# A two-layer decoder trunk on one core: block sums placed behind chosen relus, finished pairs turned earlier, and another order of the last products, roots and stores

## The chip, the cores and the metric

The kernel runs on one core of a Trainium2 chip, as a single program. The metric is the device time of the program in microseconds (us); shorter is better. The time before is the median of three runs, and one further execution was taken by the hardware profiler. An instruction belongs to one of five engines, which the profile calls PE (TensorE), DVE (VectorE), ACT (ScalarE), POOL (GpSimd) and SP (SyncE, which here only issues transfers). Each engine works through its own instructions in the order in which they were built; a scheduler fixes that order at build time, and semaphores tie the engines together.

## What is computed

The reference is a decoder trunk of two layers on 512 tokens of 1024 values, in float32:

```
for layer in range(2):
    h = rms_norm(x, norm_mix[layer])
    x = x + (short_conv_mixer(h, ...) if layer == 0 else nsa_mixer(h, ..., shared))
    x = x + squared_relu_mlp(rms_norm(x, norm_mlp[layer]), mlp_w1[layer], mlp_w2[layer])
    if layer == 0:
        shared = nsa_shared_kv(rms_norm(x, kv_norm), ...)
return rms_norm(x, final_norm)

def squared_relu_mlp(h, w1, w2):          # w1: 1024 x 4096, w2: 4096 x 1024
    return square(relu(h @ w1)) @ w2
```

The first layer mixes with a short gated convolution, the second with sparse attention over keys and values that are computed once. The change touches the two MLPs and the final norm only.

## The kernel before, in words

**Numbers.** Every float32 operand of a product is split into a high and a low half in float16, and a product is three matmuls (high by high, high by low, low by high). A weight arrives by a transfer into a float32 staging buffer (`wst`); ScalarE makes its high half (`whi`) and VectorE its low half (`wlo`). The residual `X` lies turned, channels on the partitions, in 8 tiles of 128 channels by 512 tokens.

**The MLP.** It is done in two halves of 2048 hidden units. `mlp_up` (L487) computes a half's hidden units in 8 pairs of 128-row tiles. A pair is 48 matmuls of 512 columns (L341 to L343). What follows them is a chain over the engines: two relus on VectorE (L499, with the norm's root as a row `rb` multiplied in), one square on ScalarE (L501), four sums of 128x256 on POOL (L503), the high half `rh` on ScalarE (L504) and the low half `rl` on VectorE (L505). The four sums form the seven combinations in which a 2x2 block product needs only seven products instead of eight; `rh` and `rl` hold all seven for the down products.

`mlp_down` (L538) runs over 4 pairs of output tiles. A pair takes 8 pieces of hidden units, each with 7 products of three matmuls of 256 columns (L550 to L552). The weights come as blocks: a staging buffer holds two pieces, VectorE forms the weights' combinations in place with four sums (L182, the list `W_SUMS`), ScalarE makes the high half of all seven combinations (L184, 128x1792) and VectorE the low half (L185, 128x1792). `combine` (L508) turns the seven sums in PSUM into additions to `X`: one ScalarE copy `dn_p` (L520), two VectorE operations that make `dn_w`, then a generator of seven more VectorE operations, which `mlp_down` advances one step behind every piece of the next pair.

**Which weights are ready when.** All weights stand in one list of pieces in the order of their use. `ahead` (L215) is called behind a pair's weights or a block's first piece; it converts pieces until 2 (for blocks 3) are ready beyond those in use. Staging buffers: 3 for plain pieces and 3 for blocks; converted ones: 4 and 4. `convert_piece` (L171) ends by starting the transfers for which a staging buffer has come free, on SP's queue. So a half's first three blocks are loaded, summed and split while the last up pairs still run. Nothing in the kernel says where among the up pairs they stand on VectorE: the scheduler places them, by when it expects their data and their engine.

**The root of the MLP's norm.** Sums of squares of `X` are gathered while `X` is made; in the first half's first up pair, four small matmuls add them over the partitions, and `rstd_of` (L295 to L305) makes the reciprocal root by a square root on ScalarE and five VectorE operations that refine it. Four transposes (L312) spread it into `rb`, which the first relu needs.

**The end.** In the last down phase (layer 1, half 1) each finished pair of output tiles is turned back to token-major form while the next pair is computed. `mid_b` calls `token_major` (L1168) for both halves of the tokens behind piece 5 of the next pair: TensorE transposes (L1166), ScalarE squares with an accumulating sum (L1162), ScalarE copies (L1177) into `xt` (the tiles `xsh` and `xsl`, 4 x 128 tokens), and POOL multiplies by the final norm's gain (L1178). At that place on ScalarE they stand, in the order built, behind the conversions of four blocks. The last output pair is `last_b` (L1205): its seven products are run one behind the other, each with its own additions (through the helper `stt`, L1213), then the last transposes, and `store` (L1188) makes two tokens tiles' root, scales them with ScalarE (L1195) and VectorE, and starts the transfer to the output on SP's queue (L1203): one per 128 tokens, whole rows.

The order on TensorE is the order of the program's text. Lines of the profile are those of the kernel before.

Of the kernel before, what the change touches and what calls it, by code (L numbers as in the profile page):

```python
# [48 lines left out]
def body(ctx, tc, x, rel_bias, norm_mix, norm_mlp, mlp_w1, mlp_w2, a_w_in, a_conv_w, a_w_out,  # L49
# [121 lines left out]
    def convert_piece(step=1024):  # L171
# [7 lines left out]
        if shape is None:  # L179
            b = t.rearrange("p (k b n) -> p k b n", k=2, n=128)  # L180
            for e, o, x, y in W_SUMS:
                DVE.tensor_tensor(b[:, :, o], b[:, :, x], b[:, :, y], op=e)  # L182
# [303 lines left out]

    def mlp_up(xs, ss, rh, half, rb):  # L487
        turn[0] = 1
        for p in range(8):
# [8 lines left out]
            for m in range(2):  # L498
                DVE.scalar_tensor_tensor(t[:, m], ph[m], 0.0, rb, op0=OP.max, op1=OP.mult)  # L499
# [6 lines left out]
        return rb  # L506

    def combine(p, acc7, done):  # L508
# [11 lines left out]
        ACT.activation(p1, P1, AF.Copy, scale=sc)  # L520
# [17 lines left out]
    def mlp_down(rh, done, mid=None, last=None):  # L538

        post = iter(())  # L540
        for p in range(4):
# [13 lines left out]
            for c in range(0, 4 if late else 8, 2):  # L555
                w = next_piece()
                for k in range(2):
                    for i in range(7):
                        product(i, c + k, [u[:, k] for u in w])
                    if c + k == 5 and mid:  # L560
                        mid(p)
                    if k == 0:
                        drain(ahead())
                    next(post, None)
# [8 lines left out]
            post = combine(p, acc7, done)  # L573
        drain(post)
# [570 lines left out]
    with pool("hidden_b") as hp:  # L1145
# [22 lines left out]
        def token_major(p, h, tag):  # L1168
# [4 lines left out]
            for i in range(2):  # L1173
# [3 lines left out]
                ACT.activation(o, v, AF.Copy)  # L1177
                POOL.tensor_tensor(o, o, gains(p), op=OP.mult)  # L1178

        def mid_b(p):  # L1180
            if p:
                for h in range(2):
                    token_major(p - 1, h, "a" if p % 2 else "c")
# [4 lines left out]
        def store(h, late=None):  # L1188
            sst = work.tile([128, 2], F32, name="sst", bufs=2)
            DVE.tensor_reduce(sst, ssf[:, 2 * h:2 * h + 2], axis=mybir.AxisListType.X, op=OP.add)  # L1190
            r = rstd_of(sst)
            for i in range(2):
                t = 2 * h + i
                a, b = xt[t][:, 0:512], xt[t][:, 512:1024]
                ACT.activation(a, a, AF.Copy, scale=r[:, i:i + 1])  # L1195
                if late:
                    b = xt[t][:, 512:768]
                    DVE.scalar_tensor_tensor(xt[t][:, 768:896], late[i], r[:, i:i + 1], gains(3, 1),
                                             op0=OP.mult, op1=OP.mult)
                    c = xt[t][:, 896:1024]  # L1200
                    DVE.tensor_scalar(c, c, r[:, i:i + 1], None, op0=OP.mult)
                DVE.tensor_scalar(b, b, r[:, i:i + 1], None, op0=OP.mult)
                nc.sync.dma_start(out[0, t * 128:(t + 1) * 128, :], xt[t])  # L1203

        def last_b(acc7, product):  # L1205
# [16 lines left out]
            DVE.tensor_tensor(X1[:, n1], X1[:, n1], p1, op=OP.add)  # L1222
# [61 lines left out]
```

## Time and profile before

| what | us |
|---|---|
| median of 3 runs | 1137.51 (1137.13 to 1138.04) |
| the profiled execution's own time | 1136.88 |
| its span, first to last instruction | 1135.1 |
| matmuls of a 512-column tile, mean (L341 to L343) | 0.379 |
| four POOL sums L503, all 128 | 99.9 in all, 0.801 each |
| high halves of blocks on ScalarE L184, 64 | 106.9 in all, 1.692 each |
| low halves of blocks on VectorE L185, 64 | 128.8 in all, 2.019 each |
| weight sums on VectorE L182, 256 | 108.9 in all, 0.469 each |
| `rl` on VectorE L505, 32 | 64.8 in all, 2.026 each |

The page gives each engine's busy time and its share of the span, the span in 40 slices, the transfers, the chain of work that ended last, and the costliest groups of instructions. A row of a timeline is: start and duration in us, engine, line, operation, output <- inputs with their shape and type, how many alike in a row, and in brackets how long the engine was idle just before and what ended that. A duration there is that of the instruction from start to end; two in a row may overlap by about 0.1 us, so "step" below means the distance from one start to the next. A matmul's duration is longer than its step: 512 columns take 0.38 from start to end, and follow each other every 0.22. Times in the text that name no row are differences of such starts.

### The profile page before, as it was taken

Reading aid. Unit: us, or ns where it says so; the run is one execution under the profiler, and the core shown is the slowest. Engines: PE = TensorE matmul, PEld = TensorE weight load, DVE = VectorE, ACT = ScalarE, POOL = GpSimd, SP = SyncE. Lnnn points to the kernel's source line nnn. Section 1 sums busy time; section 2 is a strip of 40 time slices with the busy share of each in tenths; the row PEclk is TensorE's granted clock in tenths of the full one; section 3 lists DMA queues with packets and bytes.
Section 4 is the critical chain, followed back from the end, with each engine's and each line's share of the span. In section 5 each row is a group of like instructions: output and inputs, shape, how many; then the busy total and the mean of one; then the engine's idle time right before and its main releaser. Section 6 shows DMA issues by size and latency. Waiting matters only on the chain.

```text
span 1135.1 us, 20099 instructions
## 1 busy us (share of the span) xinstructions
PE 1095.8 (97%) x7959; PEld 694.1 (61%) x7959; DVE 832.3 (73%) x1498; ACT 568.5 (50%) x922; POOL 157.6 (14%) x198
## 2 busy tenths in 40 slices
PE   8999999999999999999999989899999999999985
PEld 4444444446884448865767666664444787445874
DVE  4755458765897556999589969896895598754795
ACT  4532235444433444556679777765544433343452
POOL 0000000422000221001002022220122100123020
PEclk9999999999999999999999999999999999999998
DMA  6433335333333333313334341112633333330221
GB/s 210 130 94 97 107 105 172 113 93 113 112 112 112 111 95 107 112 42 120 112 78 122 83 138 38 39 38 74 187 111 112 111 109 115 105 95 7 84 84 75
DMA packets 149378, 115.75 MB, mean 102 GB/s; under 512 B 8612, under 2 KB 146564, under 8 KB 149284
## 3 DMA queue, kind: packets, MB, share of 16 engines
q1 hardware_dynamic: 146736, 109.47, 31.8%
q10 hardware_dynamic: 2260, 4.40, 1.3%
q8 instruction: 62, 1.02, 0.4%
q0 software_dynamic: 288, 0.61, 0.2%
q14 instruction: 32, 0.26, 0.1%
HBM read 110.22 MB, written 2.14 MB: 99 GB/s over the span
## 4 chain that ended last, share of the span: by engine, by line
PE 50%; DVE 19%; ACT 11%; issue 7%; POOL 7%; DMA 5%; SPq 1%; DVEq 0%; ACTq 0%; POOLq 0%
POOL ml_z L503 6%; PE a L341 4%; PE a L342 4%; PE a L343 4%; DVE wlo L185 4%; DMA wst<-mlp_w_dram 3%; ACT rh L504 3%; PE c L343 3%; PE c L342 3%; PE c L341 3%; PE b L342 3%; PE b L341 3%; PE b L343 3%; DVE wlo L196 3%; DVE ml_t L499 2%
## 5 line engine op out<-in xcount | busy, mean ns | idle before, releaser
L195 ACT ACTIVATE whi<-wst 128x1024 f16<-128x1024 f32 (+4 forms) x171 | 142.4, 858 | 127.9 <-PE b L342 38.4
L196 DVE SCALAR_TENSOR_TENSOR wlo<-wst,whi 128x1024 f16<-128x1024 f32 (+4 forms) x171 | 169.9, 1001 | 40.2 <-ACT whi L195 39.9
L503 POOL TENSOR_TENSOR ml_z<-ml_z 128x256 f32<-128x256 f32 x128 | 99.9, 801 | 610.1 <-ACT ml_z L501 410.1
L184 ACT ACTIVATE whi<-wst 128x1792 f16<-128x1792 f32 x64 | 106.9, 1692 | 135.4 <-DVE wst L182 102.3
L341 PEld LDWEIGHTS <-whi 128*128 128x128 f16 x1024 | 100.4, 98 | 112.3 <-issue 5.5
L343 PEld LDWEIGHTS <-wlo 128*128 128x128 f16 x1024 | 100.2, 98 | 112.1 <-issue 0.4
L342 PEld LDWEIGHTS <-whi 128*128 128x128 f16 x1024 | 100.2, 98 | 107.6 <-issue 2.0
L505 DVE TENSOR_TENSOR rl<-ml_z,rh 128x1792 f16<-128x1792 f32 x32 | 64.8, 2026 | 135.9 <-ACT rh L504 135.7
L185 DVE SCALAR_TENSOR_TENSOR wlo<-wst,whi 128x1792 f16<-128x1792 f32 x64 | 128.8, 2019 | 3.0 <-ACT whi L184 2.9
L182 DVE TENSOR_TENSOR wst<-wst 128x256 f32<-128x256 f32 x256 | 108.9, 469 | 24.4 <-DMA wst<-mlp_w_dram 23.4
L504 ACT ACTIVATE rh<-ml_z 128x1792 f16<-128x1792 f32 x32 | 54.3, 1698 | 106.1 <-POOL ml_z L503 106.1
L551 PEld LDWEIGHTS <-whi 128*128 128x128 f16 x896 | 87.7, 98 | 16.2 <-issue 5.6
L552 PEld LDWEIGHTS <-wlo 128*128 128x128 f16 x896 | 87.6, 98 | 15.0 <-issue 4.2
L550 PEld LDWEIGHTS <-whi 128*128 128x128 f16 x896 | 87.7, 98 | 10.5
L343 PE MATMUL b<-xsh,wlo 128*128 128x512 f16 x208 | 78.8, 379 | 0.0
L342 PE MATMUL b<-xsl,whi 128*128 128x512 f16 x208 | 78.8, 379 | 0.0
L341 PE MATMUL b<-xsh,whi 128*128 128x512 f16 x208 | 78.7, 379 | 0.0
L501 ACT ACTIVATE ml_z<-ml_t 128x1024 f32<-128x1024 f32 x32 | 33.8, 1057 | 88.4 <-DVE ml_t L499 88.4
L963 ACT ACTIVATE at_p<-at_s,at_m 128x128 f32<-128x128 f32 (+3 forms) x128 | 71.0, 557 | 13.7 <-DVE at_m L961 12.6
L551 PE MATMUL a<-rl,whi 128*128 128x256 f16 x256 | 69.8, 273 | 3.7 <-DVE rl L505 3.7
L341 PE MATMUL c<-xsh,whi 128*128 128x512 f16 x192 | 72.8, 379 | 0.0
L342 PE MATMUL c<-xsl,whi 128*128 128x512 f16 x192 | 72.8, 379 | 0.0
(309 smaller groups left out, 2686.4 us busy)
## 6 DMA issues: line engine op xcount, KB each, us to landing
wst<-mlp_w_dram SPq DMA_DIRECT2D x256, 256.0 KB, 3.3
wst<-a_w_in_dram SPq DMA_DIRECT2D x18, 512.0 KB, 3.5
wst<-w_kv_dram SPq DMA_DIRECT2D x12, 512.0 KB, 3.5
T<-ext_d ACTq DMA_DIRECT2D x4, 1056.0 KB, 6.0
wst<-a_w_out_dram SPq DMA_DIRECT2D x8, 512.0 KB, 3.4
wst<-b_w_qg_dram SPq DMA_DIRECT2D x8, 512.0 KB, 3.5
wst<-b_w_o_dram SPq DMA_DIRECT2D x8, 512.0 KB, 3.3
wst<-a_w_in_dram SPq DMA_DIRECT2D x8, 384.0 KB, 5.5
```

The lines of the kernel that those rows point to most:

```text
L182: DVE.tensor_tensor(b[:, :, o], b[:, :, x], b[:, :, y], op=e)
L184: ACT.activation(hi, b[:, :, 1:], AF.Copy, scale=sc)
L185: DVE.scalar_tensor_tensor(lo, b[:, :, 1:], sc, hi, op0=OP.mult, op1=OP.subtract)
L195: ACT.activation(hi[:, s:e], w, AF.Copy, scale=sc)
L196: DVE.scalar_tensor_tensor(lo[:, s:e], w, sc, hi[:, s:e], op0=OP.mult, op1=OP.subtract)
L341: PE.matmul(ps, w[0], xs[0], start=start, stop=False)
L342: PE.matmul(ps, w[0], xs[1], start=False, stop=False)
L343: PE.matmul(ps, w[1], xs[0], start=False, stop=stop)
L503: POOL.tensor_tensor(z[:, o], z[:, a], z[:, b], op=e)
L504: ACT.activation(rh[0][:, p], z[:, 1:8], AF.Copy)
L550: PE.matmul(acc7[i], wh, xh, start=c == 0 and not other, stop=False, skip_group_check=other)
L551: PE.matmul(acc7[i], wh, xl, start=False, stop=False, skip_group_check=other)
```

## The change

Four things are changed.

- **Block sums behind a relu.** A list `hold` takes the second relu of up pairs 2, 4 and 6 of each half. When the next block is converted, its four sums are ordered behind the relu that stands first in the list (`issue_after` keeps the order on VectorE; it is no wait). Which operations then follow is again up to the scheduler. There are three relus and three blocks ahead.
- **Finished pairs at once.** In `mlp_down`, the call that converts further weights (`drain(ahead())`) is ordered behind an instruction: at a pair's first piece behind the copy `dn_p` of the pair before (`copied`), and in the last down phase, at piece 5, behind the last copy of the turned tokens (`mid` now returns it). There, the block of pieces 4 and 5 calls it at its second piece instead of its first. `combine` is advanced one step directly when it is made, and no longer at piece 0.
- **The last pair.** `last_b` runs the product for P5 before that for P7, with their additions. The first two token tiles' gain and root are no longer applied by `store`: `root` makes a root, and for tiles 0 and 1 one VectorE operation applies gain and root to the last 256 columns straight from PSUM and another the root to columns 0 to 767; both stand behind the last addition (`final`) on VectorE. ScalarE no longer scales those two tiles.
- **The stores.** `put` starts a transfer: whole rows of tiles 0 and 1 on SP's queue, then tiles 2 and 3 in two halves of the columns, the first on ScalarE's queue behind its scaling, the second on SP's.

```diff
@@ convert_piece
-            for e, o, x, y in W_SUMS:
-                DVE.tensor_tensor(b[:, :, o], b[:, :, x], b[:, :, y], op=e)
+            with tc.issue_after(hold.pop(0).ins) if hold else nullcontext():
+                for e, o, x, y in W_SUMS:
+                    DVE.tensor_tensor(b[:, :, o], b[:, :, x], b[:, :, y], op=e)
@@ mlp_up
+    hold = []
...
-                DVE.scalar_tensor_tensor(t[:, m], ph[m], 0.0, rb, op0=OP.max, op1=OP.mult)
+                relu = DVE.scalar_tensor_tensor(t[:, m], ph[m], 0.0, rb, op0=OP.max, op1=OP.mult)
+            if p in (2, 4, 6):
+                hold.append(relu)
@@ combine
-        ACT.activation(p1, P1, AF.Copy, scale=sc)
+        copied[0] = ACT.activation(p1, P1, AF.Copy, scale=sc)
@@ mlp_down
-                    if c + k == 5 and mid:
-                        mid(p)
-                    if k == 0:
-                        drain(ahead())
-                    next(post, None)
+                    behind = None
+                    if c + k == 0 and p:
+                        behind = copied[0]
+                    if c + k == 5 and mid and p:
+                        behind = mid(p)
+                    if k == (1 if c == 4 and mid else 0):
+                        with tc.issue_after(behind.ins) if behind else nullcontext():
+                            drain(ahead())
+                    if c + k or not p:
+                        next(post, None)
...
             post = combine(p, acc7, done)
+            next(post)
@@ token_major, mid_b
-                ACT.activation(o, v, AF.Copy)
+                last = ACT.activation(o, v, AF.Copy)
                 POOL.tensor_tensor(o, o, gains(p), op=OP.mult)
+            return last
...
-            if p:
-                for h in range(2):
-                    token_major(p - 1, h, "a" if p % 2 else "c")
+            return [token_major(p - 1, h, "a" if p % 2 else "c") for h in range(2)][1]
@@ store becomes root and put
+        def root(h):
+            sst = work.tile([128, 2], F32, name="sst", bufs=2)
+            DVE.tensor_reduce(sst, ssf[:, 2 * h:2 * h + 2], axis=mybir.AxisListType.X, op=OP.add)
+            return rstd_of(sst)
+
+        def put(t, queue, at=slice(0, D)):
+            queue.dma_start(out[0, t * 128:(t + 1) * 128, at], xt[t][:, at])
@@ last_b
+            product(4)
+            stt(both, P5[:, None, :].to_broadcast([128, 2, 256]), both)
             product(3)
             stt(wv[:, 0], P7, wv[:, 1])
             DVE.tensor_tensor(both, both, wv, op=OP.add)
-            product(4)
-            stt(both, P5[:, None, :].to_broadcast([128, 2, 256]), both)
...
-                DVE.tensor_tensor(xt[t][:, 768:1024], ps[:, 0:256], gains(3), op=OP.mult)
-            store(0)
+                early.append(ps[:, 0:256])
+            r = root(0)
...
-                DVE.tensor_tensor(xt[t][:, 896:1024], ps[:, 0:128], gains(3)[:, 128:256], op=OP.mult)
+                early.append(ps[:, 0:128])
             product(6)
-            stt(X2[:, n1], P4, X2[:, n1])
+            final = DVE.scalar_tensor_tensor(X2[:, n1], P4, sc, X2[:, n1], op0=OP.mult, op1=OP.add)
...
-            store(1, late)
+            with tc.issue_after(final.ins):
+                for t in range(2):
+                    DVE.scalar_tensor_tensor(xt[t][:, 768:1024], early[t], r[:, t:t + 1], gains(3),
+                                             op0=OP.mult, op1=OP.mult)
+                    DVE.tensor_scalar(xt[t][:, 0:768], xt[t][:, 0:768], r[:, t:t + 1], None, op0=OP.mult)
+                    put(t, nc.sync)
+            r = root(1)
+            for i in range(2):
+                t, c = 2 + i, r[:, i:i + 1]
+                ACT.activation(xt[t][:, lo], xt[t][:, lo], AF.Copy, scale=c)
+                put(t, nc.scalar, lo)
+                DVE.scalar_tensor_tensor(xt[t][:, 768:896], late[i], c, gains(3, 1), op0=OP.mult, op1=OP.mult)
+                DVE.scalar_tensor_tensor(xt[t][:, 896:1024], early[t], c, gains(3)[:, 128:256],
+                                         op0=OP.mult, op1=OP.mult)
+                DVE.tensor_scalar(xt[t][:, 512:768], xt[t][:, 512:768], c, None, op0=OP.mult)
+                put(t, nc.sync, hi)
```

More of the change, by code (lines that the diff above doesn't have):

```diff
@@ L1 @@
 import math
-from contextlib import ExitStack
+from contextlib import nullcontext, ExitStack
 import numpy as np
@@ L506, in mlp_up @@
         return rb
+    copied = [None]
     def combine(p, acc7, done):
@@ L1232, in last_b @@
             stt(X1[:, n1], P2, X1[:, n1])
+            lo, hi = slice(0, 512), slice(512, 1024)
+            early = []
             for t in range(2):
```

14 lines of the change are left out of this document (removed).

## Prediction

> **What bounds the kernel now.** The page is read first, then the list of what TensorE waited for, then the engines' timelines around each wait.
>
> ```profile
> span 1135.1 us, 20099 instructions
> PE 1095.8 (97%) x7959; PEld 694.1 (61%) x7959; DVE 832.3 (73%) x1498; ACT 568.5 (50%) x922; POOL 157.6 (14%) x198
> ```
>
> TensorE is busy in 97% of the span. The change takes no product away, so it can only move the 39 us in which TensorE is idle, and the end after the last product. The waits of TensorE that lie in the two MLPs:
>
> ```profile
> PE a L551 <- DVE rl L505: 3.7, 3, 1.8
> PE a L550 <- ACT xsh L1177: 2.5, 1, 2.5
> ...
> PE e L312 <- DVE rs_r L305: 1.8, 2, 0.9
> ...
> PE c L1166 <- DVE X L1213: 1.5, 1, 1.5
> ...
> PE c L550 <- DVE dn_w L1213: 0.8, 1, 0.8
> PE a L1166 <- DVE X L531: 0.6, 1, 0.6
> ...
> PE a L550 <- ACT xsl L1177: 0.5, 1, 0.5
> PE c L550 <- ACT xsl L1177: 0.5, 1, 0.5
> PE c L550 <- ACT xsh L1177: 0.4, 1, 0.4
> ```
>
> Columns: waiter, releaser, us in total, times, longest. They sum to 12.3 us; these are what the change can win or make longer. The first row is three of the four turns from the up to the down products; the timeline of VectorE, then of TensorE, shows why.
>
> ```profile
> 264.92 1.28 DVE L499 SCALAR_TENSOR_TENSOR ml_t<-b,rb 128x512 f32<-128x512 f32 x2
> ...
> 272.03 2.03 DVE L505 TENSOR_TENSOR rl<-ml_z,rh 128x1792 f16<-128x1792 f32 x1 [4.70 <-ACT rh L504]
> 273.98 1.22 DVE L196 SCALAR_TENSOR_TENSOR wlo<-wst,whi 128x1024 f16<-128x1024 f32 x1
> 275.11 1.28 DVE L499 SCALAR_TENSOR_TENSOR ml_t<-c,rb 128x512 f32<-128x512 f32 x2
> ```
> ```profile
> 255.83 0.38 PE L343 MATMUL b<-xsh,wlo 128*128 128x512 f16 x1
> ...
> 266.19 0.38 PE L343 MATMUL c<-xsh,wlo 128*128 128x512 f16 x1
> ...
> 282.45 0.27 PE L550 MATMUL a<-rh,whi 128*128 128x256 f16 x1
> 284.31 0.27 PE L551 MATMUL a<-rl,whi 128*128 128x256 f16 x1 [1.58 <-DVE rl L505]
> ```
>
> The relu (L499), square, four POOL sums, `rh` and `rl` (L505) are a chain, and VectorE runs in order, so the next relu stands behind this `rl`. The chain turns once in 10.19 us (264.92 to 275.11), TensorE's pair in 10.36 (255.83 to 266.19). A relu that is late therefore wins back only 0.17 us a pair. Here it starts 8.92 us behind its pair's last product (275.11 - 266.19). `rl` ends 9.15 us after its relu's start (264.92 to 272.03 + 2.03), at 18.1. TensorE has 16.4 us of products that don't need it (to 282.56, one step after 282.45) and waits for the rest. **So the wait at a turn is lag + 9.15 - 16.4**, and each us put into the chain is a us of waiting once the lag is over 7.2.
>
> **Part 1: the block sums.** The built order of the changed program says where they now stand. In each half, behind the relus of pairs 2 and 4: one sum (L182), the up weights' low half, three sums, `rl`, a block's low half (L185), another up low half, the next relu. Behind pairs 3 and 5: four sums before `rl`. Behind pair 6: four sums, `rl`, two block low halves, the last relu. Behind that: eight sums and two up low halves ahead of the last `rl`. Sums fall into VectorE's 4.70 us of idleness, but POOL's sums run in the same time. The rows of POOL in pairs 0, 2 and 3, and of VectorE in pair 2, price that; then the block low halves and sums by themselves:
>
> ```profile
> 201.19 5.64 POOL L503 TENSOR_TENSOR ml_z<-ml_z 128x256 f32<-128x256 f32 x4 [197.56 <-DMA wst<-mlp_w_dram]
> ...
> 226.03 3.47 POOL L503 TENSOR_TENSOR ml_z<-ml_z 128x256 f32<-128x256 f32 x4 [7.96 <-ACT ml_z L501]
> 236.80 2.90 POOL L503 TENSOR_TENSOR ml_z<-ml_z 128x256 f32<-128x256 f32 x4 [7.29 <-ACT ml_z L501]
> ```
> ```profile
> 226.25 4.00 DVE L182 TENSOR_TENSOR wst<-wst 128x256 f32<-128x256 f32 x5
> ...
> 352.77 2.02 DVE L185 SCALAR_TENSOR_TENSOR wlo<-wst,whi 128x1792 f16<-128x1792 f32 x1
> 354.70 1.76 DVE L182 TENSOR_TENSOR wst<-wst 128x256 f32<-128x256 f32 x5
> ```
>
> Five sums take 1.76 us alone and 4.00 beside POOL, whose four go from 2.90 to 3.47: +0.57 in the chain per pair with sums. Its bounds: 0, where they miss each other, and +2.7, the 5.64 of pair 0. I take 0.57, since four of the pairs repeat pair 2's picture. A block low half between `rl` and relu adds its step, 1.93 (352.77 to 354.70). The Trainium skill ("SBUF — State Buffer", Who interferes with whom) says that a VectorE operation with two SBUF inputs and a POOL operation that reads SBUF exclude each other for the whole instruction. The trace agrees (4.00 against 1.76), and the rule speaks against this change; the sum would be the same by it.
>
> Per half: pairs 2 and 4 gain 2 x (0.57 + 1.93) = 5.0, pairs 3 and 5 2 x 0.57 = 1.1. Pair 6: its up low half now stands behind three sums and reaches 1 us into POOL's time (+0.9), two block low halves (+3.9), one up low half fewer before the relu (-1.14, 273.98 to 275.11): +3.6. Less 5 x 0.17: **+8.9 of lag**. The last `rl`: POOL's 0.57, and VectorE, with eight sums and two low halves, is free only at 8.2 us instead of 7.1: +1.1 (half 1, with shorter low halves: +0.8).
>
> What lag do the halves start from? Half 0: the first relu waits for the weights' high half, released by pair 0's last product:
>
> ```profile
> 192.34 1.06 ACT L195 ACTIVATE whi<-wst 128x1024 f16<-128x1024 f32 x1 [3.05 <-PE b L342]
> ```
>
> With its low half (1.22 in the rows above) behind it the relu starts at 194.6, 2.4 behind pair 0's last product, which is issued just ahead of this row; two pairs and the root's four transposes (0.5 of TensorE's time, by the eight of L1166 below) bring pair 2 to 1.6. Turn: 1.6 + 8.9 + 9.15 + 1.1 - 16.4 = **4.4 us**, in each layer. Half 1: the sums of its first blocks leave the end of the down phase and the relu's front (354.70 is one such row), so the lag starts at 0.4, a product's own 0.38. Turn: 0.4 + 8.9 + 9.15 + 0.8 - 16.4 = **2.9**. In layer 1's half 1 pairs 2 to 4 gain 5.6; behind pairs 5 and 6 no up low half follows (-1.14 each), and in pair 6 a block's low half holds POOL's last sum back (1.95), a second one (1.93) and two sums (0.7) precede the relu: -0.6 and +3.4. Lag 0.4 + 5.6 - 0.6 + 3.4 - 0.85 = 8.0, `rl`, with 0.4 of POOL, at 17.6, wait **1.2**. Together 4.4 + 4.4 + 2.9 + 1.2 = 12.9 where 3.7 stood: **+9.2**.
>
> Loads on SP's queue: blocks' loads now stand between up loads, each behind a low half; the up load next in the queue needs the staging buffer of the low half directly behind, so nothing waits longer. POOL's own order doesn't change.
>
> **Part 1b: the root.** Before, a block's low half sits inside the root's chain:
>
> ```profile
> 190.75 0.17 DVE L301 RECIPROCAL rs_r<-rs_r 128x4 f32<-128x4 f32 x1
> 190.83 1.99 DVE L185 SCALAR_TENSOR_TENSOR wlo<-wst,whi 128x1792 f16<-128x1792 f32 x1
> ...
> 193.56 0.15 DVE L305 SCALAR_TENSOR_TENSOR rs_r<-rs_t,rs_r 128x4 f32<-128x4 f32 x1
> ```
>
> Without it and the sums the root is there by 191, before TensorE asks. Both waits for `rs_r` go: **-1.8**; next is TensorE itself.
>
> **Part 2: finished pairs.** In the last down phase ScalarE now copies the turned tokens behind the second conversion instead of the fourth:
>
> ```profile
> 1076.26 3.29 ACT L184 ACTIVATE whi<-wst 128x1792 f16<-128x1792 f32 x2 [3.18 <-DVE wst L182]
> ```
> ```profile
> 1072.79 1.04 PE L1166 MATMUL a<-ident,X 128*128 128x128 f32 x8
> ...
> 1080.87 0.27 PE L550 MATMUL a<-rh,whi 128*128 128x256 f16 x1 [2.46 <-ACT xsh L1177]
> ...
> 1111.84 1.06 PE L1166 MATMUL a<-ident,X 128*128 128x128 f32 x8 [0.59 <-DVE X L531]
> ```
> ```profile
> 1081.43 1.39 DVE L182 TENSOR_TENSOR wst<-wst 128x256 f32<-128x256 f32 x2 [1.41 <-DMA wst<-mlp_w_dram]
> ...
> 1111.02 0.68 DVE L531 TENSOR_TENSOR X<-X,dn_w 128x512 f32<-128x512 f32 x1
> ```
>
> The tokens are turned by 1073.8, so the copies end by 1076.5 instead of 1082 and the four waits on `xsh` and `xsl`, 3.9 us, go. The conversions queued behind them on ScalarE have their sums at about 1076 anyway. But what is late next is VectorE: between 1081.43 and the sum at 1111.02, which releases the transposes, it has hardly a pause. Its work there is the same after: 20 sums x 0.34, 7 low halves x 1.93 and twice nine instructions of a pair's combining, some 3.5: 27 us. It can begin up to 1.4 us sooner (the idleness in its row), and its sums beside POOL (0.70 each in that row) fall into that pause: about 1.1. That pulls the transposes **2.5** earlier, not 3.9; bounds 0.8 (the load is late again) and 4.5. On the other side the last `rl` of the up phase, at 17.6 instead of 15.97 behind the last up product, makes VectorE's work **1.6** later.
>
> **Part 3: the end.** P7 follows P5, so 0.77 us of waiting for `dn_w` hide behind a product of 1.3:
>
> ```profile
> 1116.84 0.27 PE L550 MATMUL c<-rh,whi 128*128 128x256 f16 x1 [0.77 <-DVE dn_w L1213]
> ```
> ```profile
> 1126.15 1.32 ACT L1195 ACTIVATE xsh<-xsh,rs_r 128x512 f32<-128x512 f32 x2
> ```
> ```profile
> 1129.95 1.05 SPq L1203 DMA_DIRECT2D out_dram<-xsl  x2
> ```
>
> ScalarE's two scalings (1.32) no longer stand ahead of the last square. Four VectorE instructions stand ahead of the second root's sum instead, but start as soon as the first root is there: 0.9 less by my count. From the stores' issue to the span's end stay 5.2 us (1129.95 to 1135.1). Sum of the end: **-1.7**, bounds 0 and -2.5. The store on ScalarE's queue and the 768-wide scaling have no row; I take SP's store and 1.5 times a 512-wide one, and the bounds hold twice that.
>
> **Sum.** -1.8 + (9.2 - 1.2, the last turn being counted with VectorE) + 1.6 - 2.5 - 1.7 = +3.6 us against the profiled execution's own 1136.88 (span 1135.1 and 1.8 around it). That lies 0.6 below the median of the runs, 1137.51, so I forecast 1141.1.
>
> **Rivals.**
> *The sums hide (faster).* The mechanism: if sums and POOL miss each other in the pairs 2 to 6, the chain keeps 2.90 and only the block low halves lengthen it. Lag then grows by 4 x 1.93 - 1.14 - 0.85 = 5.7 instead of 8.9; half 0 turns at 7.4, half 1 at 6.1, either side of the 7.2 that decides, and the waits of 3.7 shrink to 0.4. -1.8 - 3.3 - 2.5 - 1.7 = -9.3: 1128.2. For it: four sums take 1.4 us of 4.70 idle. Against it: 3.47 in pair 2.
> *The end gives all (no change).* If VectorE keeps up in the last down phase, all of 3.9 + 0.6 goes instead of 2.5 and the last `rl` costs 1.2 instead of 1.6: 2.4 less, 1138.7.
> *The clock falls.* A wait of 4.4 us might halve TensorE's clock.
>
> ```profile
> 715.00:718.00 3.00, 2.91 (x22) 2.79 (x23) 2.29 (x4) 1.79 (x4) 1.27 (x1) 0.50 0.02 5
> 1078.00:1081.00 3.00, 0.54 (x6) 0.33 (x5) 2.02 (x1) 3.00 (x9) 0.74 (x2) 1.00 0.37 124
> ```
>
> Columns: stretch, us, busy us of PE, PEld, DVE, ACT, POOL, granted clock, DMA share, GB/s. 3 us at half clock, behind a thin stretch, cost 1.5; a 2.46 us wait didn't halve it. Two turns so struck: 1144.1. The Trainium skill ("TensorE: Matmul & The Clock Gate", What's actually happening) gives the gate a window of about 3.4 us; the trace lets both stand.
>
> **How the numbers follow.** The forecast 0.50, the sums hide 0.22, the end gives all 0.18, the clock 0.10. The range takes in the hidden sums and two struck turns with a little on top: 1127.5 to 1146. 0.2% is 2.3 us, about what a measurement tells from no change. Faster is the first rival: 0.22. Within: the second and a tenth of the forecast's own spread: 0.23. Slower: the rest, 0.55.
>
> **What would show it.** In the profile after: POOL's L503 rows of pairs 2 to 5 near 3.5 with sums beside them (2.9 proves the first rival); relus 12.7 us apart behind pairs 2 and 4; waits of TensorE on `rl` summing to about 13 us in four turns; none on `rs_r`; none on `xsh`; one of 2 us or more on the transposes of the last down phase; granted clock 1.00 after each turn. The forecast is wrong if the relus' spacing stays under 11.

## The result and the profile after

The changed kernel takes 1142.42 us (median of 9 runs, 1139.38 to 1147.55); the kernel before, in 9 runs, 1136.95 (1135.42 to 1138.39). The ratio is 1.0052 (95% interval 1.0035 to 1.0069): 5.5 us slower, half a per cent, with the whole interval above 1. The profiled execution's own time is 1142.42, its span 1140.6.

The first lines of the page of the kernel after:

```profile
span 1140.6 us, 20066 instructions
PE 1101.8 (97%) x7959; PEld 697.7 (61%) x7959; DVE 850.7 (75%) x1496; ACT 567.3 (50%) x920; POOL 165.5 (15%) x198
```

The span grew by 5.5, and TensorE's busy time by 6.0 with the same 7959 products. So not all of the loss is waiting: some products took longer. What TensorE waited for in the kernel after, in the MLPs (waiter, releaser, us in total, times, longest):

```profile
PE a L558 <- DVE rl L510: 6.8, 3, 2.7
PE a L1179 <- DVE X L538: 2.5, 1, 2.5
...
PE a L557 <- ACT rh L509: 1.9, 2, 1.0
...
PE a L559 <- DVE wlo L186: 1.9, 2, 1.5
...
PE c L1179 <- DVE X L1250: 0.7, 1, 0.7
...
PE c L559 <- DVE wlo L186: 0.4, 1, 0.4
```

(Lines moved: L505 is now L510, L499 L502, L501 L506, L503 L508, L504 L509, L531 L538, L550 to L552 L557 to L559, L182 L183, L184 L185, L185 L186, L1166 L1179, L1213 L1250.) The waits on the root and on `xsh` and `xsl` are gone. The wait on `rl` has grown from 3.7 to 6.8, one on `rh` has joined it, and a low half of block weights (`wlo`), which TensorE never waited for by more than 0.2, is now late.

Where the time lies, by the end of the last product of each stage in both profiled executions (us from the span's start; the last column is what the stage itself gained or lost):

| stage | before | after | difference |
|---|---|---|---|
| layer 0, first up half | 266.57 | 265.19 | -1.38 (0.28 of it in the start) |
| layer 0, first down half | 341.67 | 343.89 | +3.60 |
| layer 0, second up half | 424.55 | 426.77 | 0 |
| layer 0, second down half | 498.87 | 504.28 | +3.19 |
| attention and layer 1, first up half | 882.64 | 887.64 | -0.41 |
| layer 1, first down half | 957.98 | 966.43 | +3.45 |
| layer 1, second up half | 1040.86 | 1049.31 | 0 |
| layer 1, second down half | 1124.01 | 1130.65 | -1.81 |
| the end | 1135.1 | 1140.62 | -1.12 |

The row of the attention holds two things: layer 1's first up half by itself is 1.13 us shorter (84.29 instead of 85.42), the attention ahead of it 0.73 longer. The change doesn't touch the attention; over all profiled kernels it takes 297.3 to 299.6 us, with stretches at half clock in some. The second up halves run at TensorE's pace in both. Three down phases lose 10.2 us: in the first halves at or just behind the turn, in layer 0's second half partly at low halves further on. VectorE's relus and POOL's sums in layer 0's first half, kernel after, pairs 2 to 7:

```profile
214.70 1.28 DVE L502 SCALAR_TENSOR_TENSOR ml_t<-a,rb 128x512 f32<-128x512 f32 x2
...
227.40 1.28 DVE L502 SCALAR_TENSOR_TENSOR ml_t<-b,rb 128x512 f32<-128x512 f32 x2
...
237.64 1.28 DVE L502 SCALAR_TENSOR_TENSOR ml_t<-c,rb 128x512 f32<-128x512 f32 x2
...
250.34 1.28 DVE L502 SCALAR_TENSOR_TENSOR ml_t<-a,rb 128x512 f32<-128x512 f32 x2
...
260.58 1.28 DVE L502 SCALAR_TENSOR_TENSOR ml_t<-b,rb 128x512 f32<-128x512 f32 x2
...
274.52 1.28 DVE L502 SCALAR_TENSOR_TENSOR ml_t<-c,rb 128x512 f32<-128x512 f32 x2
```
```profile
217.15 3.48 POOL L508 TENSOR_TENSOR ml_z<-ml_z 128x256 f32<-128x256 f32 x4 [7.29 <-ACT ml_z L506]
229.85 2.96 POOL L508 TENSOR_TENSOR ml_z<-ml_z 128x256 f32<-128x256 f32 x4 [9.22 <-ACT ml_z L506]
...
263.04 3.91 POOL L508 TENSOR_TENSOR ml_z<-ml_z 128x256 f32<-128x256 f32 x4 [7.29 <-ACT ml_z L506]
276.96 3.48 POOL L508 TENSOR_TENSOR ml_z<-ml_z 128x256 f32<-128x256 f32 x4 [10.02 <-ACT ml_z L506]
```

TensorE ends a pair every 10.36. The relus are 12.70, 10.24, 12.70, 10.24 and 13.94 apart: behind pairs 2, 4 and 6 the chain loses 2.3, 2.3 and 3.6, and behind 3 and 5 it wins back only 0.1. POOL's four sums take 3.48 where block sums run beside them from the start, 2.96 where those come late, 3.91 where an up low half lies across the first. So the last relu starts 9.7 us behind the start of its pair's last product (8.92 before), its chain takes 10.29 instead of 9.15, and TensorE waits at the turn; its rows with a wait there, and then the clock behind it:

```profile
282.23 0.27 PE L557 MATMUL a<-rh,whi 128*128 128x256 f16 x1 [1.00 <-ACT rh L509]
284.86 0.27 PE L558 MATMUL a<-rl,whi 128*128 128x256 f16 x1 [2.36 <-DVE rl L510]
```
```profile
282.00:284.00 2.00, 0.27 (x1) 0.10 (x1) 2.00 (x2) 2.00 (x3) 0.00 (x0) 1.00 0.01 2
284.00:286.00 2.00, 1.14 (x11) 1.02 (x11) 2.00 (x2) 2.00 (x2) 0.00 (x0) 1.00 0.91 257
286.00:289.00 3.00, 3.00 (x17) 2.09 (x15) 2.67 (x2) 1.20 (x2) 0.00 (x0) 0.50 0.24 68
289.00:292.00 3.00, 3.00 (x28) 2.57 (x27) 1.16 (x4) 0.00 (x0) 0.00 (x0) 0.93 0.81 246
```

Columns: stretch, us, busy us (and instructions) of PE, PEld, DVE, ACT, POOL, then granted clock, DMA share, GB/s. After 3.36 us of waiting with one product between, TensorE gets back to work at 284.86, and from 286.0 its clock is 0.50 for 3.4 us: 17 products in 3 us instead of 28. Summed over the steps that are longer than the usual 0.109, this costs 1.7 us here and 1.5 behind the same turn of layer 1. The page before had no such stretch in the MLPs.

### The profile page after: what moved, and what is told of

Read it like the earlier page. It is cut to its first block, busy times and chain, and to the rows that moved or that the text cites. A ratio compares the mean times of both kernels' runs of the same rounds, so it can differ in the third digit from the quotient of the medians.

```text
span 1140.6 us, 20066 instructions
## 1 busy us (share of the span) xinstructions
PE 1101.8 (97%) x7959; PEld 697.7 (61%) x7959; DVE 850.7 (75%) x1496; ACT 567.3 (50%) x920; POOL 165.5 (15%) x198
## 4 chain that ended last, share of the span: by engine, by line
PE 49%; DVE 20%; ACT 10%; POOL 8%; issue 6%; DMA 5%; SPq 1%; DVEq 0%; ACTq 0%; POOLq 0%
POOL ml_z L508 7%; DVE wlo L186 5%; PE a L342 4%; PE a L343 4%; PE a L344 4%; ACT rh L509 4%; DMA wst<-mlp_w_dram 3%; DVE wlo L197 3%; PE b L343 3%; PE b L342 3%; PE b L344 3%; PE c L344 3%; PE c L343 3%; PE c L342 3%; DVE ml_t L502 3%
## 5 line engine op out<-in xcount | busy, mean ns | idle before, releaser
L508 POOL TENSOR_TENSOR ml_z<-ml_z 128x256 f32<-128x256 f32 x128 | 103.3, 827 | 612.6 <-ACT ml_z L506 417.0
L185 ACT ACTIVATE whi<-wst 128x1792 f16<-128x1792 f32 x64 | 106.8, 1690 | 104.8 <-DVE wst L183 83.4
L183 DVE TENSOR_TENSOR wst<-wst 128x256 f32<-128x256 f32 x256 | 125.2, 530 | 34.0 <-DMA wst<-mlp_w_dram 33.0
L186 DVE SCALAR_TENSOR_TENSOR wlo<-wst,whi 128x1792 f16<-128x1792 f32 x64 | 128.5, 2018 | 4.2 <-ACT whi L185 3.8
L510 DVE TENSOR_TENSOR rl<-ml_z,rh 128x1792 f16<-128x1792 f32 x32 | 64.8, 2024 | 79.4 <-ACT rh L509 79.4
L509 ACT ACTIVATE rh<-ml_z 128x1792 f16<-128x1792 f32 x32 | 54.3, 1697 | 107.3 <-POOL ml_z L508 107.3
L559 PEld LDWEIGHTS <-wlo 128*128 128x128 f16 x896 | 88.1, 98 | 22.7 <-issue 7.3
L557 PEld LDWEIGHTS <-whi 128*128 128x128 f16 x896 | 88.1, 98 | 11.0
L976 ACT ACTIVATE at_p<-at_s,at_m 128x128 f32<-128x128 f32 (+3 forms) x128 | 70.7, 554 | 13.9 <-DVE at_m L974 12.9
L344 PE MATMUL c<-xsh,wlo 128*128 128x512 f16 x192 | 72.8, 379 | 0.0
```

The source lines that it names most:

```text
L185: ACT.activation(hi, b[:, :, 1:], AF.Copy, scale=sc)
L186: DVE.scalar_tensor_tensor(lo, b[:, :, 1:], sc, hi, op0=OP.mult, op1=OP.subtract)
L344: PE.matmul(ps, w[1], xs[0], start=False, stop=stop)
L508: POOL.tensor_tensor(z[:, o], z[:, a], z[:, b], op=e)
L509: ACT.activation(rh[0][:, p], z[:, 1:8], AF.Copy)
L557: PE.matmul(acc7[i], wh, xh, start=c == 0 and not other, stop=False, skip_group_check=other)
```

## Experiments

**The theory.** The block sums and low halves lengthen the chain; the lag that they leave is waited for at the turns; a long wait is followed by a stretch at half clock. **The rivals.** The loss of the second halves comes from the conversions that are ordered behind the copy of P1; the clock falls for a reason of its own; VectorE, and not the chain through POOL, is the limit. Kernels of one group ran on the same chip; each group has its own runs of the kernel before beside it.

**Taking the change apart.** Four kernels, with 1137.7 for the kernel before. The first is the changed kernel without these two lines:

```diff
-            if p in (2, 4, 6):
-                hold.append(relu)
```

> The changed kernel without the ordering of the block sums; finished pairs, last products, roots and stores as changed. The theory: the three turns cost 3.6, 3.2 and 3.4 us more only because of the sums' place, by waits on rl and rh, by two stretches at half clock behind the long waits, and in half 1 by late low halves. They go and the two waits on the root (2.2) come back: 1142.4 - 10.2 + 2.2 = 1134.4; granted clock 0.995, no stretch at half clock, and the spread of the runs as small as before. The rival: half 1's 3.2 come from the conversions that were ordered behind the copy of P1; they stay, 1137.6.

Measured: 1136.3, ratio 0.999 (0.998 to 1.000), 1.4 under the kernel before; expected were 2.6 under. The turns of layer 0 are as they were in the kernel before (waits of 1.52 and 0.21), at layer 1's first turn nothing is left to wait for, layer 0's second down half takes 74.55 instead of 77.67, and the sums' place is thus the whole loss. The rest of the changes give less than expected; two of its waits, on the root in layer 1 (2.29) and on the sum ahead of the last transposes (2.51), were each followed by a stretch at half clock.

The second is the kernel before with only the block sums ordered (`hold`, the two lines above and `issue_after` in `convert_piece`).

> The kernel before with the ordering of the block sums alone. The theory: three turns +10.2, root -2.2, and a last rl that is late by 1.6 and pushes VectorE's work in the last down phase, where a wait for the turned tokens may absorb it: 1136.9 + 8.0 to 9.6 = 1145 to 1146.6, with half clock behind both half 0 turns. The rival, that the other parts make half 1's loss: 1141.8 to 1143.4.

Measured: 1144.95, ratio 1.0067 (1.0054 to 1.0079), 7.25 over the kernel before, where the theory said 8 to 9.6 over and the rival 4.9 to 6.5. The time alone lies between the two. The profile decides: its second half of layer 0 has the late low halves (waits of 0.12, 0.45, 0.37 and smaller ones, 2.85 us of idleness in the down phase against 2.88 after) without any change to `mlp_down`.

The third is the kernel before with `copied`, the order behind it, `mid`'s returned copy and the advanced `combine`.

> The kernel before with finished pairs turned at once and conversions ordered behind the copies, alone. The theory, as in the prediction: the four waits on the turned tokens (3.9) go, the transposes then wait for VectorE: -2.5, bounds -0.8 and -4.5, so 1134.4 (1132.4 to 1136.1). The rival: the conversions ordered behind the copy of P1 cost half 1 of each layer 1.5 or more, and the time is 1136 to 1138.

Measured: 1136.29, ratio 0.9989 (0.9979 to 1.0000), 1.4 less. By the time alone the rival would stand (1136 to 1138); the profile speaks against it: the second down half of layer 0 takes 74.75 against 74.49, where the rival asks for 1.5 more, and the last down half 81.11 against 83.31: -2.2, near the -2.5 of the forecast. The span of the profiled execution is 2.5 under that of before, the medians show 1.4; where the rest of them lies isn't seen in one profile. What TensorE waited for in it:

```profile
PE a L553 <- DVE rl L505: 3.9, 3, 1.8
PE e L312 <- DVE rs_r L305: 2.9, 2, 1.9
...
PE a L1174 <- DVE X L533: 2.5, 1, 2.5
```

The waits on `xsh` and `xsl`, 3.9 us, are gone, and one of 2.5 on the last pair's sums stands in their place.

The fourth is the kernel before with the new `last_b`, `root` and `put`.

> The kernel before with the last pair's products, roots and stores in the new order, alone. The theory: the wait on dn_w (0.77) goes and the end after the last product is 1.1 shorter: -1.9, 1135.0. The rival: the root's four VectorE operations ahead of the second root give it back, 1136.2; the profile then shows the second root later by 0.8 or more.

Measured: 1135.92, ratio 0.9984 (0.9975 to 0.9993), 1.8 less, as expected. In its waits there is none on `dn_w`, and the end behind the last down half is 1.08 shorter.

Alone, the last two parts win 1.4 and 1.8; together, in the first kernel, 1.4. In that kernel's one profile the two stretches at half clock and a low half that came 1.45 late stand against them.

**The long waits and the clock.** In the changed kernel, 14 products that nothing reads go into the turns of the first halves. The first form, in part:

```diff
+                    for _ in range(14 if fill and p == 0 and c + k == 7 else 0):
+                        PE.matmul(bank("e"), fill[0][:, 0, 0:128], fill[0][:, 0], start=True, stop=True)
                     for i in range(7):
                         product(i, c + k, [u[:, k] for u in w])
```

> The changed kernel, and in both half 0 turns 14 products of 512 columns (14 x 0.216 = 3.0 us) into an unused bank, issued ahead of the last piece's products, where TensorE waits 3.4 us; their results are not used. The theory: a wait of over 3 us costs itself and then a stretch at half clock (1.6 us of lost products in layer 0, 1.4 to 2.6 in layer 1); with TensorE busy the clock stays at 1.00 and 3 to 4 us go: about 1139. The rival: the clock is lowered for another reason and stays so whatever TensorE does; then the time is that of the changed kernel, 1142.4 to 1143, with granted clock 0.50 in the profile some 4 us after the turn.

Measured: 1148.86, ratio 1.0102 (1.0088 to 1.0115). It settles nothing: the scheduler put the added products one by one between the waiting ones, so the waits stayed (0.89 and 2.15 in layer 0) and the added time came on top. The second form holds them together, as one accumulation, each behind the one ahead of it (again in part; the last piece's products are ordered behind them):

```diff
+                    if fill and p == 0 and c + k == 7:
+                        ps = bank("e")
+                        for j in range(14):
+                            with tc.issue_after(end.ins):
+                                end = PE.matmul(ps, fill[0][:, 0, 0:128], fill[0][:, 0], start=j == 0, stop=j == 13)
```

> As the kernel with 14 unused products in each half 0 turn, but with these now held together, in front of the last piece's products, as one accumulation in an unused bank (before, they stood one by one between the waiting products, so that the wait stayed and 6 us of products came on top). 14 x 0.216 = 3.0 us of products stand in a wait of 3.4 to 3.6. The theory: the long wait is what lowers the clock; the turns now show waits under 0.7 and no granted clock of 0.50 behind them, and 1.6 to 2.6 us a turn go: 3 to 4 us under the changed kernel. The rival: the clock falls whatever stands in the wait; time as the changed kernel, 0.50 behind the turns.

Measured: 1140.11, ratio 1.0012 (1.0000 to 1.0023); the changed kernel beside it 1142.22, ratio 1.0036 (1.0022 to 1.0050). That is 2.1 less, not 3 to 4. TensorE in layer 0's turn, then the clock of both turns, in the kernel with the products held together:

```profile
281.28 3.19 PE L569 MATMUL e<-xsh 128*128 128x512 f16 x14
284.30 0.27 PE L557 MATMUL a<-rh,whi 128*128 128x256 f16 x1
```
```profile
284.00:286.00 2.00, 1.33 (x11) 0.87 (x9) 2.00 (x2) 2.00 (x3) 0.00 (x0) 1.00 0.78 232
286.00:289.00 3.00, 3.00 (x30) 2.70 (x28) 3.00 (x2) 1.59 (x2) 0.00 (x0) 1.00 0.20 47
...
905.00:908.00 3.00, 3.00 (x30) 2.69 (x29) 2.66 (x2) 1.19 (x2) 0.00 (x0) 1.00 0.23 61
```

With 3.2 us of useless work in the wait, 30 products run in 3 us where 17 ran before, the waits that are left are 0.67 and 0.51, and the clock stays at 1.00. One profile could show that by chance, but all runs bear it out: the granted clock over the whole span is 0.996 in the median of these 11 (0.992 to 0.997) and 0.990 in the 9 of the changed kernel beside them (0.987 to 0.994). So idleness lowers the clock, and it costs a second time. The shortfall against 3 to 4 us is not settled. In the profiles the first down halves gain 1.5 and 1.7 us on those of the first profile after, and 2.5 and 2.4 on those of the next profile, where waits and half clock last longer; that such a wait goes unpunished in some executions, below, is one reason that would fit the smaller difference of the medians.

The changed kernel once more, on that chip:

> The changed kernel once more, for a profile and times on the chip of the two kernels beside it: 1142.4, waits of 3.4 to 3.6 at the half 0 turns with half clock behind them in most, but perhaps not all, executions.

Measured: 1142.22. The waits in layer 0's turn are 1.01 and 2.36 as before, but the half clock behind them lasts twice as long and costs 2.7:

```profile
284.00:290.00 6.00, 4.93 (x24) 3.41 (x24) 4.89 (x3) 3.41 (x3) 0.00 (x0) 0.50 0.55 163
290.00:293.00 3.00, 3.00 (x27) 2.56 (x26) 1.92 (x5) 0.32 (x1) 0.00 (x0) 0.90 0.59 198
```

The times of the changed kernel go with their clocks: in the first nine runs the longest, 1147.55, has a mean granted clock of 0.986, the shortest, 1139.38, of 0.993. The kernel before spreads in the same way, over 3 us in its nine runs and over 6.7 in the 25 beside these kernels, of which the longest, 1142.77, has 0.988.

**The place of the sums.** The changed kernel with other relus:

```diff
-            if p in (2, 4, 6):
+            if p in (0, 2, 4):
```

> The changed kernel with the block sums ordered behind the relus of pairs 0, 2 and 4 instead of 2, 4 and 6. The theory: what counts is the sum that the chain gets in a half, since it wins back only 0.17 us a pair; two pairs earlier gives back 0.3, and the low halves that stood ahead of the last relu and the last rl no longer add 1.1 at the turn: 1.5 to 2 us less wait a turn, so waits near 1.5 to 2, mostly without half clock: 1136 to 1139. The rival: the place right at the turn was the whole loss, and with two free pairs behind it the lag is gone: waits of 0 and 1130 to 1132.

Measured: 1141.2, ratio 1.0027 (1.0016 to 1.0039); 1.0 under the changed kernel beside it, which the intervals don't tell apart. Neither expectation holds. The waits in layer 0's first turn:

```profile
282.97 0.27 PE L557 MATMUL a<-rh,whi 128*128 128x256 f16 x1 [1.67 <-ACT rh L509]
285.03 0.27 PE L558 MATMUL a<-rl,whi 128*128 128x256 f16 x1 [1.79 <-DVE rl L510]
```

They are 3.46 instead of 3.36; half clock followed them in layer 1 and not in layer 0. VectorE's rows of pairs 4 and 5 in this kernel show why two pairs of rest don't help:

```profile
247.64 2.02 DVE L510 TENSOR_TENSOR rl<-ml_z,rh 128x1792 f16<-128x1792 f32 x1 [2.35 <-ACT rh L509]
249.58 2.02 DVE L186 SCALAR_TENSOR_TENSOR wlo<-wst,whi 128x1792 f16<-128x1792 f32 x1
251.51 1.22 DVE L197 SCALAR_TENSOR_TENSOR wlo<-wst,whi 128x1024 f16<-128x1024 f32 x1
252.65 2.02 DVE L186 SCALAR_TENSOR_TENSOR wlo<-wst,whi 128x1792 f16<-128x1792 f32 x1
254.58 1.28 DVE L502 SCALAR_TENSOR_TENSOR ml_t<-a,rb 128x512 f32<-128x512 f32 x2
```

Two block low halves and an up low half stand between `rl` and relu: 5.0 us in one pair. The lag has grown to 11.5 by pair 6 and is still 11.3 in pair 7; the last `rl`, with no sums ahead of it, ends 20.4 behind the last up product's start, against 20.0 in the changed kernel. A lag that is once there stays, as the theory has it; the expectation had left the two low halves in pair 4 out of the sum. What did go are most of the late low halves of the second half (its down phase takes 76.19 instead of 77.67), since there the last relu and `rl` now have no sums ahead of them.

**The length of the chain.** If the chain through POOL is what decides, it can be cut: its four sums on VectorE.

```diff
-                POOL.tensor_tensor(z[:, o], z[:, a], z[:, b], op=e)
+                DVE.tensor_tensor(z[:, o], z[:, a], z[:, b], op=e)
```

In the changed kernel:

> The changed kernel with the four sums of each up pair on VectorE instead of POOL. The theory: the chain's length behind the relu decides the turns. Four sums at a step of 0.34 take 1.4 instead of 2.9 and cannot collide with POOL, so the chain turns in about 8.7 where nothing is added; pairs with block sums gain 1.4 (their sums now stand between those of the chain) and pairs with a low half 1.93. By that half 0 turns with a wait of 0 to 2 instead of 3.4, without half clock: 1142.4 less 2 x (1.4 to 3.4 and 1.7) less up to 1.7 in half 1: 1132 to 1136. The rival: VectorE, and not the chain with POOL, is the limit; 44 us more on it leave the turns as they are or longer, 1142 or more.

Measured: 1121.85 (4 runs, 1121.4 to 1122.64), ratio 0.9863 (0.9848 to 0.9879): 16 us under the kernel before, and 10 below the expected range. The page's engines, what TensorE waits for longest (all of it in the attention), and VectorE in pair 1:

```profile
PE 1095.1 (98%) x7959; PEld 695.1 (62%) x7959; DVE 867.1 (77%) x1624; ACT 569.3 (51%) x920; POOL 57.0 (5%) x70
```
```profile
PE b L966 <- POOL Q L756: 2.6, 5, 0.6
PE b L966 <- DVE at_m L974: 2.1, 3, 1.3
PE c L982 <- DVE at_pl L988: 2.0, 4, 1.0
```
```profile
202.59 1.34 DVE L502 SCALAR_TENSOR_TENSOR ml_t<-c,rb 128x512 f32<-128x512 f32 x2
...
205.25 1.55 DVE L508 TENSOR_TENSOR ml_z<-ml_z 128x256 f32<-128x256 f32 x4
208.62 2.03 DVE L510 TENSOR_TENSOR rl<-ml_z,rh 128x1792 f16<-128x1792 f32 x1 [1.82 <-ACT rh L509]
210.57 1.22 DVE L197 SCALAR_TENSOR_TENSOR wlo<-wst,whi 128x1024 f16<-128x1024 f32 x1
212.95 0.69 DVE L502 SCALAR_TENSOR_TENSOR ml_t<-a,rb 128x512 f32<-128x512 f32 x1 [1.16 <-PE a L344]
```

The four sums take 1.55 on VectorE where nothing stands between them, 2.9 to 3.9 on POOL. From relu to the end of `rl` it is here 8.06 instead of 9.15, and the next relu waits for TensorE instead of the other way round. Where block sums and low halves follow, a lag still builds up, to 3.9 at the last relu; but the last `rl` of layer 0's first half ends 13.8 behind the last up product's start, within the 16.4 that TensorE has. No wait is left at any turn, on a low half, on the root or for the last pair's sums: three down phases take 73.52 each (75.26, 74.49 and 75.50 before), the last 77.35 (83.31). Against the changed kernel the four down phases are 5.4, 4.2, 5.4 and 4.2 shorter; the expectation had counted the turns and the clock, but not the low halves nor the last down phase.

The kernel before, with the same edit:

> The kernel before with the four sums of each up pair on VectorE instead of POOL. The theory: chain 1.5 shorter, so the lag falls by 1.7 a pair behind pair 3 and the waits at the turns (3.7) go; the waits on the root stay: 1137.7 - 3.7 = 1134. The rival, that VectorE is the limit: 1137.7 or more.

Measured: 1127.99, ratio 0.992 (0.9907 to 0.9932): 9.9 less, not 3.7. The waits at the turns are gone; so are those on `xsh` and `xsl`. The four down phases are 1.7, 1.0, 2.0 and 5.2 shorter in the profile, together as much as the gain; the forecast of 3.7 had left out the last of them.

The changed kernel without the order of the block sums, with the same edit:

> The changed kernel without the ordering of the block sums, and with the four sums of each up pair on VectorE instead of POOL. The theory: what the finished pairs and the end give (the 1136.3 of the kernel with those two alone) less the waits at the turns, 3.7: 1132.6. The rival: VectorE's later last rl pushes the last down phase, where it is the limit (a wait of 2.5 for the last pair's sums), and 1 to 2 us are given back: 1134.5.

Measured: 1125.0 (1123.73 to 1126.35), ratio 0.9893 (0.9877 to 0.9908): 12.9 less. Against the first of these three it lacks only the order of the block sums, and it is 3.15 slower; no run of one lies within those of the other. Its profile has 2.0 us of waits on the root, the other none; of the 3.9 us by which the two profiles differ, the up halves with the root make 2.4, the down phases none, and the attention, which the order doesn't touch, 1.6. So with the shorter chain the same lines that cost 7 us (the second kernel of the first group) earn 2 to 3.

## Why the prediction came out as it did

The sign and the mechanism were right, and 5.5 us lie near the 3.6 of the sum, but several terms were off and partly cancelled. Of the signs that it named, the relus 12.7 apart, the end of the waits on the root and on `xsh`, and a wait of over 2 us on the last transposes came. The waits at the turns sum to 8.7 us and not 13, and the clock behind them was not 1.00.

- **The root.** Forecast -1.8. Both waits are gone; the first up half is 1.10 shorter in layer 0 and 1.13 in layer 1. Right.
- **The chain in pairs 2 and 4, pair 6, the last `rl`.** Forecast +2.3 net, +3.4 net and +1.1; measured in layer 0's first half 2.34, 3.57 and 1.14 (10.29 from relu to the end of `rl`, less 9.15). Right, and the start's lag of 1.6 as well (1.7).
- **Pairs 3 and 5.** Here the step failed in size: "2 x 0.57". Their sums wait for the load of their block until 1.6 us into POOL's time, which begins at 229.85 in pair 3, so POOL's four take 2.96 instead of 3.47:

```profile
231.47 2.41 DVE L183 TENSOR_TENSOR wst<-wst 128x256 f32<-128x256 f32 x4 [1.66 <-DMA wst<-mlp_w_dram]
```

  The lag falls by 0.12 in each of them instead of growing by 0.40. That is why the prediction's own formula, with the lags and chains of the profile, gives turns of 3.6, 1.8 and 3.9 and not 4.4, 2.9 and 4.4; TensorE's rows show 3.4, 1.7 and 3.6. In layer 1's second half the forecast turn of 1.2 isn't there: pairs 2 to 4 add 4.2 instead of 5.1, the lag at the last relu is 6.6 instead of 8.0, and the last `rl` ends 16.0 behind the last up product's start, not 17.6.
- **The clock.** Counted as a rival at 0.10 with 1.5 us for each of two turns. It came true: 1.7 and 1.5 in the profiled execution, and the added products show that the wait is its cause. It should have been a part of the forecast, since the forecast's own waits were longer than those that the trace before had shown to pass unpunished.
- **Late low halves in the second half of layer 0.** Not foreseen: 1.7 us. The prediction priced what stands ahead of the last `rl`, but not that VectorE goes into the down phase with sums and two more low halves behind it, and that a low half sets a product's start there. The kernel with the sums alone shows it, the one with other relus lacks most of it.
- **Finished pairs.** Forecast -2.5, less 1.6 for a late last `rl`. By itself it gave -2.2 in its stage, with the wait of 2.5 on the last transposes that was foreseen. The 1.6 rested on a last `rl` at 17.6; it ended at 16.0, as before (15.97), so that loss was not there. By luck another stood in its place: a low half was 1.46 late. The conversions now stand behind ScalarE's copies, and VectorE's order has changed with them: four sums that wait 3.20 for their load stand ahead of two low halves, whose high halves ScalarE has ended by 1086.2 and 1088.1:

```profile
1084.09 2.29 DVE L183 TENSOR_TENSOR wst<-wst 128x256 f32<-128x256 f32 x5
1089.58 1.55 DVE L183 TENSOR_TENSOR wst<-wst 128x256 f32<-128x256 f32 x4 [3.20 <-DMA wst<-mlp_w_dram]
1091.05 3.95 DVE L186 SCALAR_TENSOR_TENSOR wlo<-wst,whi 128x1792 f16<-128x1792 f32 x2
```
```profile
1084.53 1.70 ACT L185 ACTIVATE whi<-wst 128x1792 f16<-128x1792 f32 x1
1086.41 1.70 ACT L185 ACTIVATE whi<-wst 128x1792 f16<-128x1792 f32 x1 [0.18 <-DVE wst L183]
```
```profile
1093.12 0.28 PE L559 MATMUL a<-rh,wlo 128*128 128x256 f16 x1 [1.46 <-DVE wlo L186]
```

  The kernel with the pairs alone has the same order, and there the same low half is 0.14 late. What differs is the load: from its issue to the first of these sums pass 5.4 us here, 5.2 in the kernel without the order of the block sums (low half 1.45 late) and 5.6 in the changed kernel's second profile (1.63 late), but 4.0 to 4.2 in the kernels with the pairs alone, with other relus and with added products (0 to 0.33 late). Why a load takes longer in some executions isn't shown.

- **The end.** Forecast -1.7, with 0.77 of it in the last down half. The end behind the last product is 1.12 shorter, the wait on `dn_w` is gone, and 5.2 us stay from the stores' issue (1135.45) to the span's end. Right.

The sum by what the profiles show: -1.4 and -0.4 up to the turns, waits at the turns +5.3 with the first steps behind them, clock +3.2, low halves +1.7, last down half -1.8, end -1.1: +5.5, as measured. That the forecast came within 2 us is luck: the turns, counted 2.7 too long (8.0 net), stood in for a part of the clock and the low halves, which were left out.

One number looks odd: the wait of 2.50 to 2.52 on the last pair's sums is the same in seven of these kernels, whatever the last `rl` did. The traces show why. In all seven, TensorE's product 26.26 us ahead of the transposes is released by the same low half (the row at 1093.12 above). From there on TensorE has 23.75 us of products, and VectorE runs through one fixed row of work up to `X`, with a single pause of some 1.5 us for the last block's load:

```profile
1108.43 1.90 DVE L183 TENSOR_TENSOR wst<-wst 128x256 f32<-128x256 f32 x4 [1.47 <-DMA wst<-mlp_w_dram]
```

That load is issued at 1104.44, right behind the low half that frees its staging buffer (it ends at 1104.41), and its block's sums start 4.0 us later. Whatever is late ahead of that product shows in its own wait, from 0 to 1.63, and not in the 2.5.

## What to carry to other kernels

When two engines pass work in turn, compare the time that the chain takes from one start to the next with that of its supplier: here 10.19 against 10.36, so a us put into the chain stays until the phase ends, less the 0.17 that each pair wins back, wherever in the phase it is put. Shorten such a chain before filling its gaps: the four sums took 2.9 us on the third engine, up to 3.9 with other work beside them, and 1.55 on VectorE; the same placement of work lost 7 us with the long chain and won 2 to 3 with the short one. And price a wait of TensorE with the stretch at half clock that can follow it.

## What the runs showed of the hardware

**From 2.3 us on, a wait is followed by half clock in some executions and not in others.** In the thirteen profiled executions, no single wait of TensorE in the MLPs under 1.9 us (27 of them from 0.9 us) was followed by half clock; of those from 2.3 to 2.6, 7 of 11 were; of the turns with over 3.0 us in two waits, 8 of 10, among them one of 1.67 and 1.79 us. No single wait lay between 1.9 and 2.3. The last transposes are left out, since TensorE has next to no work behind them. The stretches lasted 3.4 us (286.0 to 289.4, from the clocks 0.50 and 0.93 above) or 6.8 (the changed kernel again: 6 us at 0.50, 0.6 in the next three, 0.2 ahead). The Trainium skill ("TensorE: Matmul & The Clock Gate", What's actually happening) describes a free-running window of about 3.4 us; lengths of one and two windows, and waits of one length that are sometimes struck and sometimes not, agree with it. The Trainium skill ("TensorE: Matmul & The Clock Gate", Why this matters for your kernels) advises against idle gaps of over about 3 us; here 2.3 us were enough, and the measurement decides.

**A block's low half holds a sum on POOL back until it has ended.** Where a low half (1.93 alone) ran beside POOL's last sum, that sum took 2.39 instead of 0.72: it began 0.3 us behind the low half's start and ended 0.6 us behind its end (pair 0 of both layers' first halves in the kernel with other relus, and pair 6 of layer 1's second half in the changed kernel).
